# Chains of seven products: the copy of the sixth and seventh products' bank by ScalarE, and VectorE's add two steps later

## The chip, the cores and the metric

The kernel runs on one core of a Trainium2 chip. A core has a matrix engine (TensorE; PE in the profile, with PEld for its weight loads), a vector engine (VectorE, DVE), an activation engine (ScalarE, ACT), GpSimd (POOL) and SyncE (SP). TensorE writes its results into PSUM, which has eight banks of 512 fp32 columns here; VectorE and ScalarE read and write PSUM and the on-chip SBUF. Each engine takes its own instructions strictly in the order in which the program emits them, and waits at one until what it needs from other engines is done.

The metric is the device time in microseconds of one execution, the median of several runs.

## The reference

A decoder trunk of two layers over 512 tokens of width 1024, all in fp32. The first layer mixes tokens by dilated attention in three groups of eight heads, the second by a gated linear recurrence; a gated ConvFFN follows each. What matters here are the large products:

```
qkv = (x @ w_qkv)                     # 1024 x 9216, attention
u = causal_dwconv(x @ w_up, conv_w, conv_b)   # 1024 x 6144, each ConvFFN
g, v = u[..., :D_FF], u[..., D_FF:]
return (gelu(g) * v) @ w_down
```

## The kernel before

Every fp32 product is made of three faster ones: a weight or activation is split into a high part (`whi`, by ScalarE, L220) and the rest (`wlo`, by VectorE, L221), and TensorE adds up hi x hi, hi x lo and lo x hi. A weight passes through both engines before TensorE can use it.

Part of the queries and keys of the attention, and ten of the twelve column blocks of each ConvFFN's `w_up`, are multiplied by a scheme that makes a 2 x 2 block product of seven block products in place of eight. One such unit is a **chain** (`chain`, L1171 to L1206): seven products, each twelve matmuls of 256 columns, into two PSUM banks. The upper bank `y[0]` takes products 5 and 3 in its columns 256 to 511 and product 2 in columns 0 to 255. The lower bank `y[1]` takes products 1, 6, 7 and 4 in columns 0 to 255, one accumulated on the other. Between them the sums that the scheme needs are taken off: ScalarE copies products 1, 5 and 1+6 into two SBUF tiles `part` (`t[0]` and `t[1]`, L1193); VectorE adds `t[0]` to the whole upper bank (L1197); and after product 7 VectorE adds the fifth product's copy to the lower bank's sum and writes it into that bank's columns 256 to 511 (L1202). Product 4 is then accumulated onto columns 0 to 255, and the consumer takes the whole bank: in the ConvFFN ScalarE (L885) with two convolution taps on VectorE (L889), in the attention VectorE (L1304). In the traces the products of one chain are told apart by their right operand: `hT` for 1, 2 and 3, `T` for 5, 6 and 7, `last` for 4.

There are 56 chains: 16 in the attention, in four rounds of four, and 20 in each of the two ConvFFNs. Neighbouring chains overlap. The order is written out by hand: a table gives each product of a chain its step (`AT` for the ConvFFN, a new chain every `CYCLE` = 10 steps, `QUAD` for the attention, a new one every `APART` = 7), and steps without a product are filled with other products.

```
CYCLE = 10
AT = {1: 0, 5: 1, 2: 2, 6: 4, 3: 5, 7: 8, 4: 13}
APART, ROUND = 7, 44
QUAD = {1: 0, 5: 2, 2: 3, 6: 4, 3: 6, 7: 8, 4: 12}
```

A step that has a product is emitted by `slot` (L445): first the product, then everything that is due, then a `tick`, which lets side work go on and usually emits the next split of a weight (`pump`). `later(n, f)` makes `f` due n slots after the present one. So an evicting instruction stands in its engine's queue at the place of its slot, between the splits. In the ConvFFN the order of slots around a chain's end is 7, then 1, 5 and 2 of the next chain, then 4; step 9 of a cycle has no product.

Of the kernel before, what the change touches and what calls it, by code (L numbers as in the profile page):

```python
# [14 lines left out]
AF = mybir.ActivationFunctionType  # L15
ALU = mybir.AluOpType
# [118 lines left out]
def kernel(  # L135
# [25 lines left out]
    nc = tc.nc  # L161
# [23 lines left out]
    def gen(dt=F32, s="g"):  # L185
        return gp.tile([P, 512], dt, tag="g", name=nm(s))

    def psum(s="ps"):
        return pp.tile([P, 512], F32, tag="ps", name=nm(s))
# [232 lines left out]
    def chunk():  # L422
        i = state["next"]
        state["next"] += 1
        return i

    def take(i, j):
        while (i, j) not in units:
            before = len(units)
            pump(1)  # L430
            assert before != len(units), (i, j, state)
        return units[i, j]

    def done(n=2):
        state["live"] -= n
# [6 lines left out]
    def later(n, f):  # L442
        due.append([n, f])
# [727 lines left out]
    def chain(right, top, bottom):  # L1171

        i = chunk()
        y, t = {}, []

        def step(n):
            W = take(i, LEFT[n][0])
            b, at = {1: (1, 0), 6: (1, 0), 7: (1, 0), 4: (1, 0), 5: (0, 256), 3: (0, 256), 2: (0, 0)}[n]
            if b not in y:
                y[b] = psum()  # L1180
            dst = y[b][:, at : at + 256]
            for k in range(4):
                for q, (wa, ha) in enumerate(PASSES):
                    mm(  # L1184
                        dst, W[wa][0][:, k, :], right[n](ha, k), start=n in (1, 5) and k == q == 0,
                        stop=k == 3 and q == 2, skip_group_check=True,
                    )
            done(1)
            if n == 1:
                t.extend(gen(s="part") for _ in range(2))  # L1190
            if n in (1, 5, 6):
                to = {1: t[0][:, 0:256], 6: t[0][:, 256:512], 5: t[1][:, 0:256]}[n]
                later(1, lambda: nc.scalar.activation(to, dst, AF.Copy))  # L1193
            elif n == 3:

                def upper():
                    nc.vector.tensor_tensor(y[0], y[0], t[0], op=ALU.add)  # L1197
                    top(y[0])

                later(1, upper)  # L1200
            elif n == 7:
                later(1, lambda: nc.vector.tensor_tensor(y[1][:, 256:512], dst, t[1][:, 0:256], op=ALU.add))  # L1202
            elif n == 4:
                later(1, lambda: bottom(y[1]))

        return lambda n: lambda: step(n)  # L1206

    def seven(hT, T, begin, last, prep):
# [669 lines left out]
```

## Time and profile before

| | us |
|---|---|
| median of 3 runs | 1366.67 (1363.19 to 1368.01) |
| the profiled execution | 1369.2 |
| its span, first to last instruction | 1367.4 |
| TensorE busy | 1338.2 |
| VectorE busy | 1103.7 |
| ScalarE busy | 807.7 |

The granted TensorE clock is 0.997 over the span. An engine's busy time is the union of its instructions' durations. A row of the timeline gives start, duration, engine, line, operation, output and inputs with their shapes, the count of equal instructions that were merged, and in brackets the idle time before it with what ended that. Matmuls are pipelined: a matmul of 256 columns takes 0.28 us, and the next starts 0.11 after it.

### The profile page before, as it was taken

To read this page: it belongs to the slowest core of one execution; us is meant where nothing else is said; L and a number is where in the kernel's file an instruction comes from. 1 tells how busy PE (TensorE), PEld (TensorE's weight loads), DVE (VectorE), ACT (ScalarE), POOL (GpSimd) and SP (SyncE) were. 2 spreads that over 40 slices of the span, in tenths; PEclk is the share of its full clock that TensorE was granted. 3 is DMA by queue.
4 is the path that set the end of the run, shared out by engine and by line. 5 is a ranking of instruction groups with operands and counts; after the bars stand their busy time and mean duration, and the time that the engine had idled before them with its cause. 6 is when DMAs were issued, how large, how long until landed. Compare 5 with 4: busy or idle time off the path is not lost.

```text
span 1367.4 us, 24126 instructions
## 1 busy us (share of the span) xinstructions
PE 1338.2 (98%) x8981; PEld 1255.3 (92%) x8981; DVE 1103.7 (81%) x2173; ACT 807.7 (59%) x1690; POOL 236.4 (17%) x392
## 2 busy tenths in 40 slices
PE   9999999999999999999999999999999999999997
PEld 7888999889899999999999889978899999999996
DVE  6686888887876899988888759768899988888853
ACT  7343555454546476666666646489576667666641
POOL 0341341212120102221221002000102222221000
PEclk9999999999999999999999999999999999999999
DMA  7553454747483647777775542431446777776411
GB/s 231 184 148 123 124 188 122 214 109 227 120 243 99 263 155 155 183 179 175 169 169 146 174 164 81 151 109 54 162 149 148 178 182 181 178 181 163 165 68 62
DMA packets 70638, 214.53 MB, mean 157 GB/s; under 512 B 10816, under 2 KB 14360, under 8 KB 58744
## 3 DMA queue, kind: packets, MB, share of 16 engines
q1 hardware_dynamic: 42552, 153.34, 33.2%
q0 software_dynamic: 27120, 58.60, 21.2%
q8 instruction: 70, 1.15, 0.3%
q10 hardware_dynamic: 848, 1.05, 0.2%
q14 instruction: 48, 0.39, 0.1%
HBM read 193.99 MB, written 18.96 MB: 156 GB/s over the span
## 4 chain that ended last, share of the span: by engine, by line
PE 62%; issue 19%; DVE 11%; DMA 5%; ACT 3%; POOL 0%; DVEq 0%; POOLq 0%; ACTq 0%; SPq 0%
PE ps L1184 31%; PE acc L493 16%; PE ps L493 6%; PE v L1381 6%; DVE wlo L221 4%; DMA raw<-in_attn_w_qkv_dram 2%; DVE u L889 1%; DMA raw<-in_ffn_w_up_dram 1%; PE v L1319 1%; PE S L1527 1%; ACT whi L220 1%; DMA ft<-turned 1%; PE S L1475 1%; PE O L493 1%; DVE ps L1197 0%
## 5 line engine op out<-in xcount | busy, mean ns | idle before, releaser
L221 DVE TENSOR_TENSOR wlo<-raw,whi 128x512 fp32r<-128x512 f32 x628 | 417.4, 686 | 94.8 <-ACT whi L220 94.1
L220 ACT ACTIVATE whi<-raw 128x512 fp32r<-128x512 f32 x628 | 370.8, 624 | 153.1 <-PE acc L493 43.5
L1184 PE MATMUL ps<-T,whi 128*128 128x256 f32 x1344 | 235.6, 276 | 0.3
L1184 PE MATMUL ps<-hT,whi 128*128 128x256 f32 x1344 | 235.0, 276 | 0.0
L493 PE MATMUL ps<-hT,whi 128*128 128x512 f32 (+1 forms) x928 | 223.8, 334 | 0.2 <-ACT whi L220 0.2
L1184 PEld LDWEIGHTS ps<-T,whi 128*128 128x128 f32 x1344 | 207.4, 191 | 2.9 <-ACT part L1193 0.7
L1184 PEld LDWEIGHTS ps<-hT,whi 128*128 128x128 f32 x1344 | 204.3, 191 | 0.7 <-ACT part L1193 0.2
L1184 PE MATMUL ps<-T,wlo 128*128 128x256 f32 x672 | 185.3, 276 | 0.0
L1184 PE MATMUL ps<-hT,wlo 128*128 128x256 f32 x672 | 185.1, 275 | 0.0
L493 PEld LDWEIGHTS ps<-hT,whi 128*128 128x128 f32 x928 | 159.7, 190 | 13.9 <-ACT whi L220 0.4
L257 POOL DMA_DIRECT2D raw<-in_ffn_w_up_dram x120 | 104.2, 950 | 391.8 <-DVE wlo L221 308.8
L493 PE MATMUL ps<-hT,wlo 128*128 128x512 f32 (+1 forms) x464 | 154.3, 333 | 0.4 <-DVE wlo L221 0.4
L493 PE MATMUL acc<-whi,ahi 128*128 128x512 f32 x336 | 128.0, 381 | 1.8 <-DVE u L889 1.8
L493 PE MATMUL acc<-whi,alo 128*128 128x512 f32 x336 | 127.7, 380 | 1.7 <-DVE alo L221 1.6
L1184 PEld LDWEIGHTS ps<-T,wlo 128*128 128x128 f32 x672 | 128.2, 191 | 0.0
L1184 PEld LDWEIGHTS ps<-hT,wlo 128*128 128x128 f32 x672 | 128.2, 191 | 0.0
L493 PE MATMUL acc<-wlo,ahi 128*128 128x512 f32 x336 | 127.3, 379 | 0.0
L1193 ACT ACTIVATE part<-ps 128x256 f32<-128x256 f32 x168 | 63.9, 380 | 76.7 <-PE ps L1184 73.9
L1381 PE MATMUL v<-whi,hT 128*128 128x512 f32 x320 | 102.7, 384 | 0.0
L493 PEld LDWEIGHTS ps<-hT,wlo 128*128 128x128 f32 x464 | 88.3, 190 | 7.5 <-DVE wlo L221 0.6
L1184 PE MATMUL ps<-last,whi 128*128 128x256 f32 x448 | 79.5, 278 | 6.5 <-DVE ps L1202 6.5
L889 DVE SCALAR_TENSOR_TENSOR u<-ps,cols,u 128x511 f32<-128x511 f32 x112 | 83.5, 746 | 2.0
(227 smaller groups left out, 2453.3 us busy)
## 6 DMA issues: line engine op xcount, KB each, us to landing
raw<-in_ffn_w_up_dram SPq DMA_DIRECT2D x48, 1024.0 KB
raw<-in_attn_w_qkv_dram SPq DMA_DIRECT2D x34, 1024.0 KB
raw<-in_ffn_w_up_dram POOLq DMA_DIRECT2D x120, 256.0 KB, 5.6
raw<-in_ffn_w_down_dram SPq DMA_DIRECT2D x14, 1024.0 KB
dw<-in_ffn_w_down_dram SPq DMA_DIRECT2D x40, 256.0 KB
raw<-in_lru_w_in_dram SPq DMA_DIRECT2D x8, 1024.0 KB
turned<-T POOLq DMA_DIRECT2D x26, 256.0 KB, 2.6
ft<-turned POOLq DMA_DIRECT2D x104, 64.0 KB, 4.9
```

Source lines behind the costliest of these rows:

```text
L220: nc.scalar.activation(hi, raw, AF.Copy)
L221: nc.vector.tensor_tensor(lo, raw, hi.bitcast(F32), op=ALU.subtract)
L257: nc.gpsimd.dma_start(blocks(i)[to], plan[i][3][0][0][:, 4 * b : 4 * b + 4, :], accum_op=ALU.add)
L493: mm(dst, l[a], r[b], start=start and n == 0, stop=stop and n == 2)
L889: nc.vector.scalar_tensor_tensor(u[:, d:], ps[:, : S - d], wc, u[:, d:], op0=ALU.mult, op1=ALU.add)
L1184: mm(dst, W[wa][0][:, k, :], right[n](ha, k), start=n in (1, 5) and k == q == 0, stop=k == 3 and q == 2, skip_group_check=True,)
L1193: later(1, lambda: nc.scalar.activation(to, dst, AF.Copy))
L1319: mm(banks[t], hT[a][:, k, t * P : (t + 1) * P], two(W[b][k % 2][:, 0, :]), start=u == n == 0, stop=u == 3 and n == 5,)
L1381: mm(bank, hT[a][:, k, t * P : (t + 1) * P], two(W[b][k % 2][:, 0, :]), start=(k, a, b) == (0, 0, 0), stop=(k, a, b) == (KD - 1, 1, 0),)
L1475: mm(Sp[a // 2][:, o + lo : o + 256], q[hh][:, a * P : (a + 1) * P], k[hh][:, k0 : (a + 1) * P], start=True, stop=True)
L1527: mm(ps[:, c], q[hh][:, c], k[hh][:, c], start=True, stop=True)
```

## The change

The sum of the first, sixth and seventh products is no longer read out of PSUM by VectorE's add. One slot after product 7, where the add stood, ScalarE copies it into the free half of the tile `t[1]`. Two slots later VectorE adds the fifth product's copy to that copy, both from SBUF, and writes the result to the same columns 256 to 511 of the lower bank. All 56 chains are changed alike; nothing else is.

```diff
             elif n == 7:
-                later(1, lambda: nc.vector.tensor_tensor(y[1][:, 256:512], dst, t[1][:, 0:256], op=ALU.add))
+                p5, u7 = t[1][:, 0:256], t[1][:, 256:512]
+                later(1, lambda: nc.scalar.activation(u7, dst, AF.Copy))
+                later(3, lambda: nc.vector.tensor_tensor(y[1][:, 256:512], u7, p5, op=ALU.add))
             elif n == 4:
                 later(1, lambda: bottom(y[1]))
```

## The prediction

> **What bounds the kernel now.** I read the page first, then stretches of the span, the groups by shape, and at last the timeline of one engine at a time around a seventh product.
>
> ```profile
> span 1367.4 us, 24126 instructions
> PE 1338.2 (98%) x8981; PEld 1255.3 (92%) x8981; DVE 1103.7 (81%) x2173; ACT 807.7 (59%) x1690; POOL 236.4 (17%) x392
> ...
> 562.33:742.03 179.70, 179.70 (x1443) 176.10 (x1441) 158.72 (x256) 120.26 (x225) 38.24 (x44) 1.00 0.72 175
> 150.00:415.00 265.00, 258.69 (x1955) 248.47 (x1954) 217.48 (x493) 132.06 (x332) 68.21 (x125) 1.00 0.57 171
> ```
>
> TensorE bounds it: 29.2 us of the span are not PE. In the steady part of the first ConvFFN (15 chains; the columns are length, PE, PEld, DVE, ACT, POOL, clock, DMA) PE is never idle, so whatever makes it wait there is added to the time whole. VectorE is next, 88% busy; ScalarE is 67% busy. In the attention chains PE is idle for 6.3 us of 265.
>
> ```profile
> L1202 DVE TENSOR_TENSOR ps<-ps,part 128x256 f32<-128x256 f32 x56 | 23.8, 426 | 0.0
> L1504 DVE TENSOR_TENSOR plo<-ft,phi 128x256 fp32r<-128x256 f32 x8 | 3.3, 418 | 0.0
> L1193 ACT ACTIVATE part<-ps 128x256 f32<-128x256 f32 x168 | 63.9, 380 | 76.7 <-PE ps L1184 73.9 <-DVE plo L1504 0.9
> L885 ACT ACTIVATE u<-ps,cols,neg 128x512 f32<-128x512 f32 x40 | 31.3, 783 | 3.0 <-PE ps L1184 3.0
> L1184 PE MATMUL ps<-last,whi 128*128 128x256 f32 x448 | 79.5, 278 | 6.5 <-DVE ps L1202 6.5
> ```
>
> L1202 is the add that the change moves; there are 56, one a chain. The last row is the fourth product, which accumulates onto what L1202 read. It waited for L1202 five times, 6.5 us in all. That is everything the change could win on TensorE.
>
> **The instructions.** 56 copies come onto ScalarE, priced by L1193: 56 x 0.380 = 21.3 us. The add reads its two inputs from SBUF; the nearest row of its size is L1504, 0.418 against 0.426 us, so I keep 0.43. Neither cost lies on TensorE. In the steady part the copy stands ahead of L909, for which ScalarE waits 1.21 us (row at 584.19 below), which hides it; without that cover it would cost 0.38 a chain at most. No DMA moves, and nothing is moved past SP's or POOL's queue. The `part` buffer is held two slots longer; no row of before waits for one, so I add nothing. What matters is the place of the add and who waits for it.
>
> The Trainium skill (Perfetto Trace Analysis, Optimizing Scalar/DVE Operations) puts VectorE's access overhead at about 60 ns in SBUF and 125 ns in PSUM. By that the add would be 65 ns shorter, an estimate from the page, and the sum about 3 us smaller; the rows above show 8 ns.
>
> **Where the add comes to stand.** A slot emits one product, then what is due, then one weight split. L1202 is due one slot after the seventh product; the fourth product comes four slots after it. The new add is due three slots after, so it is emitted directly ahead of the fourth product, behind the splits of two more slots. The question is whether the fourth product waits for it: it writes columns 0 to 255 of the bank, the add columns 256 to 511.
>
> ```profile
> 584.61 0.39 PE L1184 MATMUL ps<-T,whi 128*128 128x256 f32 x2
> ...
> 584.95 0.39 PE L1184 MATMUL ps<-hT,whi 128*128 128x256 f32 x2
> ...
> 586.17 0.28 PE L1184 MATMUL ps<-hT,wlo 128*128 128x256 f32 x1
> 586.28 0.39 PE L1184 MATMUL ps<-last,whi 128*128 128x256 f32 x2
> ...
> 584.19 0.63 ACT L909 ACTIVATE u<-u 128x512 f32<-128x512 f32 x1 [1.21 <-DVE u L889]
> 584.73 0.37 ACT L1193 ACTIVATE part<-ps 128x256 f32<-128x256 f32 x1
> 584.99 0.62 ACT L220 ACTIVATE whi<-raw 128x512 fp32r<-128x512 f32 x1
> 586.49 0.39 ACT L1193 ACTIVATE part<-ps 128x256 f32<-128x256 f32 x1 [0.88 <-PE ps L1184]
> ```
>
> The copy at 586.49 takes the fifth product, columns 256 to 511 of the upper bank, finished at about 585.1. It sat idle until the second product (operand hT, columns 0 to 255 of the same bank) ended at 586.17 + 0.28. So an engine waits for whoever was ordered before it in the bank, whatever the columns. I take the same for a product behind an add: the fourth product waits. No row shows that direction, so the other answer is a rival.
>
> The Trainium skill (PSUM — Partial Sum Buffer, PSUM bank collisions raise a hardware error) has the rule that bears on that direction: PSUM is guarded by bank and quadrant, "not by address". By the rule the wait is there; by addresses alone it would not be.
>
> **What a wait costs.** VectorE's rows of two neighbouring chains (the fourth products were to start at 586.28 and, 11.99 later, 598.27):
>
> ```profile
> 584.61 0.43 DVE L1202 TENSOR_TENSOR ps<-ps,part 128x256 f32<-128x256 f32 x1
> 584.94 1.39 DVE L221 TENSOR_TENSOR wlo<-raw,whi 128x512 fp32r<-128x512 f32 x2
> 587.42 0.69 DVE L221 TENSOR_TENSOR wlo<-dw,whi 128x512 fp32r<-128x512 f32 x1 [1.09 <-ACT whi L220]
> ...
> 596.59 0.43 DVE L1202 TENSOR_TENSOR ps<-ps,part 128x256 f32<-128x256 f32 x1
> 596.92 0.68 DVE L221 TENSOR_TENSOR wlo<-raw,whi 128x512 fp32r<-128x512 f32 x1
> 597.52 0.69 DVE L913 TENSOR_TENSOR u<-u,u 128x512 f32<-128x512 f32 x1
> 598.12 0.69 DVE L221 TENSOR_TENSOR wlo<-raw,whi 128x512 fp32r<-128x512 f32 x1
> ...
> 598.27 0.39 PE L1184 MATMUL ps<-last,whi 128*128 128x256 f32 x2
> ...
> 549.77 0.43 DVE L1202 TENSOR_TENSOR ps<-ps,part 128x256 f32<-128x256 f32 x1
> 551.31 0.68 DVE L221 TENSOR_TENSOR wlo<-raw,whi 128x512 fp32r<-128x512 f32 x1
> ...
> 550.25 0.49 PE L1184 MATMUL ps<-last,whi 128*128 128x256 f32 x2 [1.41 <-DVE ps L1202]
> ```
>
> First kind: the second L221 ends at 586.33; it can't come earlier, since its whi ends at 584.99 + 0.62. The add starts 0.10 before that end, as neighbours here overlap, and ends at 586.66. The row at 550.25 shows the product 0.05 behind the add it waits for: 586.71, so 0.43 late. Second kind: the three instructions behind L1202 move forward by the 0.33 that it held (596.59 to 596.92), so the last ends at 598.48; the add, 0.10 before that, ends at 598.81; 0.05 on is 598.86, so 0.59 late. The row at 550.25 also shows what a restart costs: two products take 0.49 in place of 0.39, 0.10 more.
>
> Does VectorE catch up while TensorE waits? What comes next in its chain:
>
> ```profile
> 575.53 0.28 PE L1184 MATMUL ps<-last,wlo 128*128 128x256 f32 x1
> ...
> 575.85 0.79 ACT L885 ACTIVATE u<-ps,cols,neg 128x512 f32<-128x512 f32 x1
> 576.53 0.61 ACT L220 ACTIVATE whi<-raw 128x512 fp32r<-128x512 f32 x1
> ...
> 577.25 0.69 DVE L221 TENSOR_TENSOR wlo<-raw,whi 128x512 fp32r<-128x512 f32 x1
> ```
>
> ScalarE's L885 starts 0.04 after the fourth product ends, L220 behind it, and VectorE takes L220's result 0.11 later. So a late fourth product makes VectorE late too, but for some 0.08, and the next wait comes again: 0.35 and 0.51, with restarts 0.45 and 0.61, 1.06 for two chains. If VectorE were not held, one wait would pay for the next and two chains would cost 0.59 + 0.10 = 0.7.
>
> **The sum.** Sixteen chains of each ConvFFN (third to eighteenth) are of this kind: 8 x 1.06 = 8.5 us. The first two start behind a full VectorE queue: the second's L221 ends at 551.99 (L1202's 0.33 leaves ahead of it, the first chain's add comes in), its own add 0.33 later, then 0.05, so 552.37 against 550.25: 2.1 for both. The nineteenth:
>
> ```profile
> 753.58 1.29 DVE L221 TENSOR_TENSOR wlo<-raw,whi 128x512 fp32r<-128x512 f32 x2
> ...
> 754.01 0.39 PE L1184 MATMUL ps<-last,whi 128*128 128x256 f32 x2
> ...
> 240.12 0.69 DVE L315 TENSOR_TENSOR raw<-raw 128x512 f32<-128x512 f32 x1
> ...
> 238.66 0.39 PE L1184 MATMUL ps<-last,whi 128*128 128x256 f32 x2
> ...
> 309.97 0.69 DVE L319 TENSOR_TENSOR raw<-raw 128x512 f32<-128x512 f32 x1
> ...
> 309.40 0.28 PE L1184 MATMUL ps<-last,whi 128*128 128x256 f32 x1
> ...
> 275.06 0.50 PE L1184 MATMUL ps<-last,whi 128*128 128x256 f32 x2 [2.01 <-DVE ps L1202]
> 343.83 0.38 PE L1184 MATMUL ps<-last,whi 128*128 128x256 f32 x1 [1.26 <-DVE ps L1202]
> ```
>
> 754.87 + 0.33 + 0.05 is 1.24 late; less 0.08, with restart, 1.3. The twentieth's add falls behind its fourth product: nothing. One ConvFFN: 8.5 + 2.1 + 1.3 = 11.9, both 23.8 us.
>
> Attention has 16 chains in four rounds. The instruction behind which the add stands gives 240.81 + 0.38 - 238.66 = 2.5 us late for the chain at 238.66, and 310.66 + 0.38 - 309.40 = 1.6 for the one at 309.40. The same reading of every chain gives nine that wait, 0.9 to 2.5 each, some 14 before any catching up and 15 with restarts; the fourth chain of a round has nothing queued between and doesn't wait longer. In rounds two and three the fourth chain waited already (2.01 and 1.26, last rows): there the lost time is partly what is lost now. Following these waits along each round I come to an estimate of 3.2, 3.3, 2.1 and 1.7, so 10; the bounds are 3, if most is swallowed by such waits and by transfers of weights, and 15. I take 9, near the estimate.
>
> Together 33 us. The profiled execution took 1369.2 us for its span of 1367.4, 2.5 over the median of the three, 1366.67; a difference goes onto either. **1366.7 + 33 = 1399 us.**
>
> **Rivals.**
> - *Columns decide, not banks.* The fourth product waits for the copy alone and the 6.5 us of waits go: 1360 us, the faster side. It decides from the first chain on. Against it stands the copy at 586.49; for it, that no row shows a product behind an add to other columns. 0.08.
> - *VectorE catches up.* Two chains cost 0.7, the ConvFFNs 2 x (5.6 + 3.4) = 18, attention 3: 1388 us. For it: VectorE is idle 1.09 before 587.42. Against: that idle ends by whi, behind the copy at 586.49, not by the add. 0.20.
> - *ScalarE's order.* The new copy waits for the seventh product and holds the splits behind it where ScalarE runs ahead, in attention; 0.38 for each of 16 chains more: 1405 us. 0.08.
> - *The add is in time*, because VectorE runs earlier than I read: 1367 us. It needs half a microsecond in every chain. 0.06.
>
> **How the numbers follow.** My forecast has 0.58, for 1390 to 1410. What this kernel's measurement can tell from no change is about 0.3%, 4 us. Slower: 0.58 + 0.20 + 0.08 = 0.86; same 0.06; faster 0.08. The range 1380 to 1412 leaves out the two cheap cases, 0.14, and a little of the tails.
>
> **What would show it.** Right: the groups name a wait of the fourth product (operand last) for the new add's line, some 30 us over about 45 chains, its matmuls 0.1 longer at each; the steady stretch grows from 179.7 by about 8 us; ScalarE gains 56 copies of 0.38 and TensorE's wait for them is near nothing. Wrong: fourth products that start while the add still runs (the first rival), or waits in every second chain alone (the second). A clock under 1.00 or longer matmuls in the steady stretch would mean that I looked in the wrong place.

## The result and the profile after

The change makes the kernel slower: 1404.28 us, median of 4 runs (1401.36 to 1406.68), against 1365.69 us for the kernel before beside it (4 runs). The ratio is 1.0278, with a 95% interval of 1.0259 to 1.0297. On a second chip it was 1404.67 against 1367.75, ratio 1.0270 [1.0255, 1.0285]. The span grew from 1367.4 to 1402.7 us, by 35.3, at a granted clock of 0.996 (0.997 before), so the clock isn't where the time went.

The first lines of the page of the changed kernel:

```profile
span 1402.7 us, 24204 instructions
PE 1347.5 (96%) x8981; PEld 1260.3 (90%) x8981; DVE 1108.1 (79%) x2173; ACT 830.3 (59%) x1746; POOL 236.6 (17%) x392
```

TensorE has the same 8981 matmuls, but 55.2 us of its span are idle in place of 29.2. VectorE has the same 2173 instructions; ScalarE has 56 instructions and 22.6 us more.

The groups by shape of the changed kernel, where the copy is line L1203 and the add L1204 (output, input, shapes, count, busy, mean ns, idle time before them and what ended it):

```profile
L1184 PE MATMUL ps<-last,whi 128*128 128x256 f32 x448 | 82.5, 285 | 35.4 <-DVE ps L1204 24.8 <-ACT part L1193 7.5 <-ACT whi L220 3.1
L1204 DVE TENSOR_TENSOR ps<-part 128x256 f32<-128x256 f32 x56 | 23.9, 426 | 0.6 <-ACT part L1203 0.6
L1203 ACT ACTIVATE part<-ps 128x256 f32<-128x256 f32 x56 | 21.3, 381 | 11.0 <-PE ps L1184 7.8
```

The fourth product (operand `last`) is where the idle time stands: 35.4 us in place of 6.5. The waits of TensorE split it by the instruction that came last:

```profile
PE ps L1184 <- DVE ps L1204: 24.8, 29, 2.1
PE ps L1184 <- ACT part L1193: 7.5, 16, 0.5
PE ps L1184 <- ACT whi L220: 3.1, 2, 1.7
```

That is 29 + 16 + 2 = 47 waits, one in nearly every chain. The 16 put down to a copy of ScalarE (L1193) are a question of naming: in each of them VectorE's add ended 0.15 us ahead of the product, as in those that are named for the add. The two put down to L220 are of the same kind.

The stretch of 15 chains that was 179.70 us long, between the same two products, and the attention stretch, in the windows view (length, PE, PEld, DVE, ACT, POOL, clock, DMA share, GB/s):

```profile
574.10:763.27 189.17, 183.21 (x1440) 177.22 (x1441) 160.29 (x255) 126.98 (x242) 37.38 (x43) 1.00 0.68 166
150.00:420.00 270.00, 255.73 (x1913) 245.55 (x1912) 215.20 (x488) 134.98 (x344) 68.63 (x125) 0.99 0.55 165
```

The steady stretch grew by 9.47 us, at full clock. In the attention's window TensorE is idle for 14.3 us of 270, where it was idle for 6.3 of 265. One wait of the steady stretch, in the timelines of VectorE and TensorE (the fourth product that started at 586.28 before), and the fourth products ahead of it and behind it:

```profile
598.13 0.69 DVE L221 TENSOR_TENSOR wlo<-raw,whi 128x512 fp32r<-128x512 f32 x1 [0.36 <-ACT whi L220]
598.74 0.43 DVE L1204 TENSOR_TENSOR ps<-part 128x256 f32<-128x256 f32 x1
599.97 0.69 DVE L221 TENSOR_TENSOR wlo<-dw,whi 128x512 fp32r<-128x512 f32 x1 [0.80 <-ACT whi L220]
...
586.78 0.46 PE L1184 MATMUL ps<-last,whi 128*128 128x256 f32 x2 [0.47 <-ACT part L1193]
...
598.72 0.28 PE L1184 MATMUL ps<-hT,wlo 128*128 128x256 f32 x1
599.31 0.46 PE L1184 MATMUL ps<-last,whi 128*128 128x256 f32 x2 [0.32 <-DVE ps L1204]
...
612.00 0.46 PE L1184 MATMUL ps<-last,whi 128*128 128x256 f32 x2 [0.47 <-ACT part L1193]
```

The second product's last matmul starts at 598.72. Unhindered, the fourth product would start 0.11 later; the add that stands behind a weight split runs until 599.17, and it starts at 599.31. Two things are to be read here. First, the gap from 598.72 is 0.59, but the idle time in brackets only 0.32: while the last matmul runs out alone, TensorE counts as busy. That is why the idle time of the group understates the loss and TensorE's busy time rose by 9.3 us with the same matmuls. Second, the loss is better read from the starts: 586.78, 599.31, 612.00 are 12.53 and 12.69 apart, where they were 11.98 on average (574.31, 586.28 and 598.27 before). Each pair of chains loses 0.55 + 0.71 = 1.26 us.

Added up in this manner over all 56 fourth products, the lag is 9.5 us at the end of the attention, 12.9 over the first ConvFFN and 13.0 over the second: 35.3 before rounding, the whole of the span's growth. One thing is hidden in the 9.5: the first matmul of the chains starts at 150.24 before and at 148.75 after. Counted from there, the attention's chains lost 11.0 us in this pair of traces.

### The profile page after: what moved, and what is told of

It is laid out like the page before. It is cut to its first block, busy times and chain, and to the rows that moved or that the text cites. A ratio compares the mean times of both kernels' runs of the same rounds, so it can differ in the third digit from the quotient of the medians.

```text
span 1402.7 us, 24204 instructions
## 1 busy us (share of the span) xinstructions
PE 1347.5 (96%) x8981; PEld 1260.3 (90%) x8981; DVE 1108.1 (79%) x2173; ACT 830.3 (59%) x1746; POOL 236.6 (17%) x392
## 4 chain that ended last, share of the span: by engine, by line
PE 52%; issue 22%; DVE 11%; ACT 7%; DMA 5%; POOL 1%; SPq 0%; DVEq 0%; POOLq 0%; ACTq 0%
PE ps L1184 24%; PE acc L493 13%; PE v L1383 6%; PE ps L493 5%; DVE wlo L221 4%; DVE u L889 3%; ACT whi L220 3%; ACT u L885 2%; DMA raw<-in_ffn_w_up_dram 2%; DMA ft<-turned 1%; DVE ps L1197 1%; ACT part L1193 1%; DVE ps L1204 1%; PE S L1529 1%; ACT u L909 1%
## 5 line engine op out<-in xcount | busy, mean ns | idle before, releaser
L220 ACT ACTIVATE whi<-raw 128x512 fp32r<-128x512 f32 x628 | 374.3, 624 | 142.8 <-PE ps L1184 41.1
L1184 PE MATMUL ps<-last,whi 128*128 128x256 f32 x448 | 82.5, 285 | 35.4 <-DVE ps L1204 24.8
L1193 ACT ACTIVATE part<-ps 128x256 f32<-128x256 f32 x168 | 63.7, 379 | 85.7 <-PE ps L1184 81.6
L1184 PEld LDWEIGHTS ps<-last,whi 128*128 128x128 f32 x448 | 68.4, 191 | 43.3 <-ACT whi L220 14.8
```

Source lines behind the costliest of these rows:

```text
L220: nc.scalar.activation(hi, raw, AF.Copy)
L1184: mm(dst, W[wa][0][:, k, :], right[n](ha, k), start=n in (1, 5) and k == q == 0, stop=k == 3 and q == 2, skip_group_check=True,)
```

## The experiments

The theory: the fourth product is held by the add that is emitted ahead of it in its bank, so the add's place costs the time, by 0.45 and 0.61 us in the steady chains. The rivals: the copy on ScalarE costs it; VectorE's extra distance or load costs it; the columns alone decide.

### The place alone, and the copy alone

`place_only` moves the add and makes no copy; it reads PSUM as before. (The last chain of each ConvFFN has its fourth product ahead of the moved add, so there the sum that is read holds that product too.)

```diff
-                later(1, lambda: nc.vector.tensor_tensor(y[1][:, 256:512], dst, t[1][:, 0:256], op=ALU.add))
+                later(3, lambda: nc.vector.tensor_tensor(y[1][:, 256:512], dst, t[1][:, 0:256], op=ALU.add))
```

> Before's add, still reading the sum out of PSUM, emitted three slots after the seventh product in place of one; no copy by ScalarE. Theory of the place and the bank: the fourth product waits for the add as in the changed kernel, so 1398 to 1408 us and a wait of the fourth product for line L1202 of some 25 to 35 us. Theory of the copy (the time goes with ScalarE's 56 copies): within 0.3% of before, 1362 to 1370 us.

`copy_only` leaves the add where it was and adds the copy, which nothing reads.

```diff
+                later(1, lambda: nc.scalar.activation(t[1][:, 256:512], dst, AF.Copy))
                 later(1, lambda: nc.vector.tensor_tensor(y[1][:, 256:512], dst, t[1][:, 0:256], op=ALU.add))
```

> Before with ScalarE's 56 copies added where the change has them; nobody reads the copies, and VectorE's add stays as it was. Theory of the place: 1363 to 1370 us, since 21 us of copies lie in ScalarE's idle time. Theory of the copy: most of the 38 us, 1390 us or more.

The place alone: 1401.55 us against 1366.07, ratio 1.0255 [1.0223, 1.0286]. The copy alone: 1364.61, ratio 1.0003 [0.9984, 1.0022]. The fourth product's group, first with the place alone, then with the copy alone:

```profile
L1184 PE MATMUL ps<-last,whi 128*128 128x256 f32 x448 | 84.8, 290 | 30.6 <-DVE ps L1202 30.6
```

```profile
L1184 PE MATMUL ps<-last,whi 128*128 128x256 f32 x448 | 79.6, 278 | 5.0 <-DVE ps L1204 5.0
L1203 ACT ACTIVATE part<-ps 128x256 f32<-128x256 f32 x56 | 21.5, 383 | 7.2 <-PE ps L1184 6.2
```

The copies lie wholly beside other work: 21.5 us more on ScalarE, no time that shows. The move gives nearly the whole loss, and here all of the wait is named for the add.

### The same extra work of VectorE, into the bank and into SBUF

Both kernels have ScalarE's copy, as the change has it, keep the add in its old place and do it a second time at the new one. `again_bank` writes the bank, `again_sbuf` writes a tile in SBUF that nothing reads.

```diff
                 later(1, lambda: nc.vector.tensor_tensor(y[1][:, 256:512], dst, t[1][:, 0:256], op=ALU.add))
+                later(3, lambda: nc.vector.tensor_tensor(y[1][:, 256:512], u7, p5, op=ALU.add))   # again_bank
+                later(3, lambda: nc.vector.tensor_tensor(p5, u7, p5, op=ALU.add))                 # again_sbuf
```

> Before's add at its place, ScalarE's copy, and the changed kernel's add three slots on as well, which writes the same values into the same columns of the lower bank once more. Place and bank: the fourth product waits for the second add, and VectorE has 0.33 us more ahead of it than in the changed kernel: 1404 to 1425 us. Theory that only VectorE's time at that place counts: the same as the kernel whose second add writes to SBUF.

> As the kernel with the add made twice, but the second add writes its result into the SBUF tile part (nobody reads it) and not into the bank. VectorE does the same work at the same place. Place and bank: no wait of the fourth product for it, 1365 to 1374 us (the 24 us of adds lie in VectorE's idle time but for the heads of the ConvFFNs). Theory of VectorE's time: 1400 us or more, as the kernel that writes to the bank.

Into the bank: 1409.07 us, ratio 1.0314 [1.0278, 1.0349]. Into SBUF: 1367.79, ratio 1.0004 [0.9983, 1.0026]. The groups of the two, in this order (the second add is L1205):

```profile
L1184 PE MATMUL ps<-last,whi 128*128 128x256 f32 x448 | 86.1, 293 | 35.7 <-DVE ps L1205 35.7
```

```profile
L1184 PE MATMUL ps<-last,whi 128*128 128x256 f32 x448 | 79.5, 278 | 6.9 <-DVE ps L1204 6.9
L1204 DVE TENSOR_TENSOR ps<-ps,part 128x256 f32<-128x256 f32 x56 | 23.8, 426 | 3.2 <-ACT part L1203 3.2
L1205 DVE TENSOR_TENSOR part<-part 128x256 f32<-128x256 f32 x56 | 23.4, 419 | 0.1
```

VectorE has 56 more instructions in the same place of its queue in both, 23.4 and 23.9 us. They cost nothing where they write elsewhere and 43.0 us (1409.07 - 1366.07) where they write the bank's other half. So neither VectorE's load nor its order costs the time; the wait for the bank does, though the two instructions touch different columns.

### Half the distance

`one_step` makes the add due two slots behind the seventh product in place of three.

```diff
-                later(3, lambda: nc.vector.tensor_tensor(y[1][:, 256:512], u7, p5, op=ALU.add))
+                later(2, lambda: nc.vector.tensor_tensor(y[1][:, 256:512], u7, p5, op=ALU.add))
```

> The changed kernel with the add two slots after the seventh product in place of three, so one step after the copy. In the steady part of the ConvFFN one or two splits then stand behind the add and not ahead of it: the add of the first kind of chain would end near 585.7, before the fourth product at 586.28, that of the second kind near 597.9 to 598.2 against 598.27, so the waits go or shrink to 0.1. Place and bank: 1366 to 1380 us. Theory of the copy: no change from the changed kernel, 1400 to 1408 us.

1374.85 us against 1367.25, ratio 1.0069 [1.0045, 1.0093]: one slot earlier takes away some three quarters of the loss (0.69% is left of 2.70 to 2.78%). TensorE's waits, a steady chain in the timelines, and the last chain of the first ConvFFN:

```profile
PE ps L1184 <- DVE ps L1204: 11.5, 10, 2.2
...
597.78 0.43 DVE L1204 TENSOR_TENSOR ps<-part 128x256 f32<-128x256 f32 x1
...
598.15 0.28 PE L1184 MATMUL ps<-hT,wlo 128*128 128x256 f32 x1
598.36 0.46 PE L1184 MATMUL ps<-last,whi 128*128 128x256 f32 x2
...
767.75 0.46 PE L1184 MATMUL ps<-last,whi 128*128 128x256 f32 x2 [1.84 <-DVE ps L1204]
```

In the steady chains the add is now nearly in time: in this one it ends at 598.21, and the product starts 0.21 after the matmul ahead of it, 0.10 late; in every other one the product starts 0.11 after it, not late at all. Most of the wait that is left lies at the heads and ends of the ConvFFNs: the second chain of each waits 2.23, and the twentieth, shown here, 1.84, since its add now stands ahead of its fourth product.

### The ConvFFNs alone, the attention alone

```diff
-                later(1, lambda: nc.vector.tensor_tensor(y[1][:, 256:512], dst, t[1][:, 0:256], op=ALU.add))
+                if moved:    # True in the ConvFFN's chains alone, or in the attention's alone
+                    p5, u7 = t[1][:, 0:256], t[1][:, 256:512]
+                    later(1, lambda: nc.scalar.activation(u7, dst, AF.Copy))
+                    later(3, lambda: nc.vector.tensor_tensor(y[1][:, 256:512], u7, p5, op=ALU.add))
+                else:
+                    later(1, lambda: nc.vector.tensor_tensor(y[1][:, 256:512], dst, t[1][:, 0:256], op=ALU.add))
```

> The change in the 40 chains of the ConvFFNs alone; the 16 attention chains as before. By the prediction's terms +24 us; by the shift of the fourth products in the changed kernel's profile (35.3 us in all, 9.5 of them by the end of the attention) +26 us and more for the whole of it: 1388 to 1394 us.

> The change in the 16 attention chains alone. By the prediction's term and by the shift in the changed kernel's profile +9 us: 1373 to 1378 us. If waits in the attention were swallowed by later waits, within 0.3% of before.

ConvFFNs alone: 1392.07 us, ratio 1.0188 [1.0161, 1.0215], so 25.7 us (0.0188 x 1367.25), 22.0 to 29.4. Attention alone: 1379.21, ratio 1.0087 [1.0057, 1.0118], so 11.9, 7.8 to 16.1, a little above the 1373 to 1378 us that were expected. Together 37.6, within the intervals as much as the whole change: the two parts add up. A single pair of traces is a poor measure of the attention, because the unchanged attention differs between executions. Its window in the kernel that changes the ConvFFNs alone:

```profile
150.00:415.00 265.00, 262.45 (x1978) 252.11 (x1977) 218.33 (x518) 132.23 (x335) 69.29 (x127) 1.00 0.57 170
```

TensorE is idle for 2.5 us of it, where the same attention in the kernel before left 6.3. Several traces together tell more. The table has the time from the first matmul of the chains to the fourth product of a round's last chain, then from round to round, in four traces whose attention has the add in its old place (the kernel before, `copy_only`, `again_sbuf`, the ConvFFNs alone) and in three that have the change there (the change, the change repeated below, the attention alone):

| round, us | one | two | three | four |
|---|---|---|---|---|
| add in its old place | 54.2 to 54.4 | 66.7 to 70.6 | 68.0 to 69.7 | 66.5 |
| changed | 61.3 to 63.0 | 70.0 to 71.9 | 69.3 to 69.6 | 68.2 to 68.4 |

Rounds one and four are steady enough to compare: they lose 7.0 to 8.8 and 1.7 to 1.9 us. Over all four rounds the two means are 13.7 us apart.

### What the copy adds: an instruction on TensorE's queue

The change was 35.3 us longer in its trace, the place alone 32.7. Behind the add the fourth product starts 0.15 us later in the one and 0.05 to 0.06 in the other. A view of the chains' line shows what differs, for the changed kernel (over the span, then within the wait above), and for the kernel before:

```profile
L1184 PEldq EVENT_SEMAPHORE  x94: 51/51/51, 146.7 to 1309.0; - x94
...
L1184 PEldq EVENT_SEMAPHORE  x1: 51/51/51, 599.2 to 599.2; - x1
```

```profile
L1184 PEldq EVENT_SEMAPHORE  x44: 51/51/51, 148.2 to 1269.1; - x44
```

TensorE's queue holds 50 more semaphore instructions of 51 ns ahead of weight loads. The Trainium skill (Perfetto Trace Analysis, Identifying Dependency Chains) says that an instruction that waits for several engines may get such instructions put ahead of it with the further conditions; the counts fit that. To tell whether the copy costs its 0.38 us on ScalarE or this instruction, four kernels ran on one chip: the change, the place alone, the place with a copy that nothing reads (where VectorE stays the last reader of the columns that the fourth product writes over), and one for the next part.

```diff
+                later(1, lambda: nc.scalar.activation(t[1][:, 256:512], dst, AF.Copy))
-                later(1, lambda: nc.vector.tensor_tensor(y[1][:, 256:512], dst, t[1][:, 0:256], op=ALU.add))
+                later(3, lambda: nc.vector.tensor_tensor(y[1][:, 256:512], dst, t[1][:, 0:256], op=ALU.add))   # place_copy
```

> The change once more, beside the move of the add without the copy and the move with a copy that nobody reads, all on one chip, to tell what the copy itself adds. In the traces so far the fourth product starts 0.15 us behind the add with the change and 0.05 to 0.06 with the move alone, and the products of the chains show 94 semaphore instructions ahead of their weight loads in place of 44. Theory (an extra semaphore instruction is the cost, since the fourth product now writes over columns that ScalarE read last): about 36 to 39 us over the kernel before, 2 to 3 us above the move alone. Rival (what differs is chance between executions): no difference from the move alone.

> The add moved two slots later, reading PSUM as before, without a copy. (In the last chain of each ConvFFN the moved add comes behind the fourth product, so there it reads a sum with the fourth product in it; the rest of the work is the same.) Theory: 33 to 36 us over the kernel before, 2 to 3 us below the change. Rival: the same as the change.

> The move alone and beside it ScalarE's copy one slot after the seventh product, which nothing reads; the add reads PSUM. (The last chain of each ConvFFN as in the move alone.) It has the change's work on ScalarE and the add's place, but VectorE is the last reader of the columns that the fourth product writes over. Theory (extra semaphore instruction): 44 semaphore instructions, the fourth product 0.05 to 0.06 behind the add, the time of the move alone within 1.5 us. Rival (the copy's 0.38 us on ScalarE costs the 2 to 3 us, by holding weight splits behind it): the time of the change.

| | us | runs from, to | ratio [95%] | semaphore instructions |
|---|---|---|---|---|
| the change | 1404.67 | 1402.72, 1405.82 | 1.0270 [1.0255, 1.0285] | 94 |
| the place and an unread copy | 1401.29 | 1400.65, 1402.15 | 1.0248 [1.0234, 1.0261] | 44 |
| the place alone | 1400.06 | 1398.41, 1401.75 | 1.0238 [1.0223, 1.0253] | 44 |

The place alone, in its windows and timelines (the same stretch and the same chain as above):

```profile
573.56:761.74 188.18, 183.65 (x1440) 177.16 (x1440) 160.26 (x255) 122.75 (x227) 37.39 (x43) 1.00 0.68 167
...
598.16 0.43 DVE L1202 TENSOR_TENSOR ps<-ps,part 128x256 f32<-128x256 f32 x1
...
586.18 0.49 PE L1184 MATMUL ps<-last,whi 128*128 128x256 f32 x2 [0.37 <-DVE ps L1202]
...
598.64 0.49 PE L1184 MATMUL ps<-last,whi 128*128 128x256 f32 x2 [0.22 <-DVE ps L1202]
...
611.26 0.49 PE L1184 MATMUL ps<-last,whi 128*128 128x256 f32 x2 [0.38 <-DVE ps L1202]
```

The starts are 12.46 and 12.62 apart: 0.48 and 0.64 over 11.98, 1.12 a pair. The unread copy, with the same ScalarE work as the change, has the same pair and the 44 instructions, and stands 3.4 us below the change. So the copy's time on ScalarE isn't most of it: the unread copy stands 1.2 us above the place alone, and their intervals overlap widely. The intervals of the change and of the unread copy overlap by a little (1.0255 to 1.0261), their runs do not. The distance from the change to the place alone, 4.6 us, is more than the 2 to 3 that were expected.

The traces tell it wait by wait. In the change, in its repeat and in the kernels that change one part alone, every fourth product that waits for its moved add has a semaphore instruction 0.11 us ahead of its start, and starts 0.14 to 0.15 behind the add. In the kernel before, the place alone, the unread copy and `again_bank`, none that waits has one, and they start 0.05 to 0.06 behind. `one_step` has both in one kernel: 25 products are held until 0.15 behind their add, all with the instruction, and one, at 272.76, starts 0.06 behind, without it. Where nothing is waited for, the instruction costs nothing that shows: there the product starts 0.11 after the matmul ahead, with it or without. In a steady chain it costs 0.07 (0.55 and 0.71 for 0.48 and 0.64); 47 waits make 3.3 us. No kernel was run that differs from the change in this instruction alone.

### The add behind the fourth product

`behind` keeps the copy and puts the add into the fourth product's slot, behind it and ahead of the consumer.

```diff
+                later(1, lambda: nc.scalar.activation(t[1][:, 256:512], dst, AF.Copy))
-                later(1, lambda: nc.vector.tensor_tensor(y[1][:, 256:512], dst, t[1][:, 0:256], op=ALU.add))
             elif n == 4:
+                later(0, lambda: nc.vector.tensor_tensor(y[1][:, 256:512], t[1][:, 256:512], t[1][:, 0:256], op=ALU.add))
                 later(1, lambda: bottom(y[1]))
```

> ScalarE's copy as in the change; VectorE's add emitted directly behind the fourth product (in the same slot) in place of directly ahead of it, so the fourth product waits for the copy alone and the add for the fourth product. Place and bank: the waits for the add vanish, also before's 6.5 us, and ScalarE's L885 waits for the add by some 0.6 us a chain: 1357 to 1368 us. Theory of the copy: 1400 us or more.

> The copy one slot after the seventh product, VectorE's add in the slot of the fourth product and behind it, ahead of the consumer of the bank. The fourth product then has no add ahead of it in the bank. Theory: 7 to 9 us under the kernel before (ratio 0.993 to 0.995): the five waits of 6.5 us and their restarts go, and nothing takes their place, since the consumer stands behind the fourth product anyway. Rival (the gain seen before was chance between executions): within 3 us of the kernel before.

1358.95 us against 1367.25, ratio 0.9943 [0.9918, 0.9968]; again on the other chip 1359.74 against 1367.75, ratio 0.9947 [0.9933, 0.9961]. It is faster than both kernels, by 8 us than the one before and by 45 than the change. Its groups, a stretch of 15 chains and the last 14 of them, then the same 14 of the kernel before:

```profile
L1184 PE MATMUL ps<-last,whi 128*128 128x256 f32 x448 | 78.8, 277 | 0.0
L885 ACT ACTIVATE u<-ps,cols,neg 128x512 f32<-128x512 f32 x40 | 31.3, 782 | 33.5 <-DVE ps L1204 33.5
L1204 DVE TENSOR_TENSOR ps<-part 128x256 f32<-128x256 f32 x56 | 24.0, 428 | 9.4 <-PE ps L1184 9.3
...
551.96:732.15 180.19, 179.97 (x1442) 176.20 (x1441) 161.80 (x258) 122.65 (x243) 38.21 (x44) 1.00 0.72 175
564.43:732.15 167.72, 167.72 (x1346) 164.38 (x1345) 150.79 (x241) 113.28 (x224) 35.61 (x41) 1.00 0.72 175
```

```profile
574.31:742.03 167.72, 167.72 (x1347) 164.37 (x1345) 148.26 (x239) 112.19 (x210) 35.27 (x41) 1.00 0.71 174
```

The fourth product waits for nothing now: the 6.5 us that it waited for the add before are gone. The wait has moved to the consumer, where ScalarE's L885 stands 33.5 us for the add. That costs almost nothing: in the 14 chains TensorE isn't idle at all, and they are as long as before to the hundredth. The chain ahead of them takes 12.47 us in place of 11.98, so the 15 take 180.19 where they took 179.70; TensorE waits there once for a copy of ScalarE (0.23 us, L1193, ahead of a product with operand `T`). The same chain of the second ConvFFN is as long.

## Why the prediction was right, and where its sizes were off

**The bound and the place.** Right. TensorE's idle time set the end, the add came to stand directly ahead of the fourth product, and the product waited for it across columns. The last was an inference from a copy behind a product; the trace of the change and the two adds with different destinations show the other direction. The lower bank is one tile of the program and fills one bank, so the runs don't tell whether the order is kept by tile or by bank. The Trainium skill's rule (PSUM — Partial Sum Buffer, PSUM bank collisions raise a hardware error) of guarding by bank and not by address agrees: adds into the other half of the bank cost 43 us, into SBUF nothing. Whether the chip itself would stall without the program's semaphore wasn't tried, since two engines would then touch one bank unguarded.

**The sum.** 1366.7 + 33 is 1399.7, where the forecast says 1399. The measured growth is 38.6 us (1404.28 over 1365.69), 5.6 more than the 33. Two terms were mis-sized: one wait in the ConvFFNs, worth some 2 us, and the attention, which has most of the rest.

**One wait.** The first of them is "add to product 0.05", taken from the row at 550.25. It measured 0.15 with the change, where the product had an instruction more on its queue; the restart came to 0.07 in place of 0.10. Without the copy the row was a good one: 0.05, restart 0.10, and 0.48 and 0.64 against the 0.45 and 0.61 of the prediction. With it 0.55 and 0.71, so 1.26 a pair and not 1.06. In the trace the sixteen chains of a ConvFFN lost 9.9 us where the sum has 8.5, so 2.8 us too little in both.

**No catching up.** Right. Every chain of a ConvFFN from the third to the nineteenth lost time, none paid for the next. The row at 599.97 shows why: VectorE is idle 0.80 us behind the add, for `whi`, exactly where the prediction put it.

| term, us | predicted | measured |
|---|---|---|
| steady stretch of 15 chains | about 8 | 9.47 |
| first two chains of a ConvFFN | 2.1 | 1.8 and 2.0 |
| nineteenth | 1.3 | 1.14 |
| twentieth | 0 | 0 |
| both ConvFFNs | 23.8 | 25.9 in the trace, 25.7 timed alone |
| attention | 9, bounds 3 and 15 | 11.0 in the trace from the first chain on, 13.7 between means of several traces, 11.9 timed alone |

**The attention.** The value lies within its bounds, but it is too small, and the round that missed is the first: 3.2 predicted, 7.0 to 8.8 in the traces. Its first three fourth products alone left TensorE idle for 5.75 us in the change, against 0.60 before. Which reading made the 3.2 too small stays open, since the prediction gives the rounds without their working. The fourth round is right, 1.7 for 1.7 to 1.9. The second and third (3.3 and 2.1) can't be confirmed: the unchanged attention moves there by as much as what is sought. The 9.5 at the end of the attention, counted from the start of the span, is near the 9 by luck. What held was that the fourth chains of rounds two and three stopped waiting: the waits of 2.01 and 1.26 are gone.

**The copies and the add.** Right at nothing for ScalarE's time: the copy alone costs none that shows. The rival in which ScalarE's order adds 0.38 a chain is out, though its 1405 us is nearer to the measured time than the forecast. Reading SBUF in place of PSUM, and still writing PSUM, didn't shorten the add: 0.426 both times; writing SBUF too, it took 0.419. The 65 ns that the Trainium skill's figures would give (Perfetto Trace Analysis, Optimizing Scalar/DVE Operations) do not show.

**The rivals.** "Columns decide" is out, but its price was good: 6.5 us of waits gone, 1360 us. The kernel with the add behind the product gets just that, 1358.95 and 1359.74, by order and not by columns. "VectorE catches up" (1388) and "the add is in time" (1367) are out; the second shows what it would have taken, since one slot earlier the steady chains are in time but for 0.10.

## What to carry to other kernels

In this kernel, where two engines share a PSUM bank, an instruction waits for what was emitted ahead of it in that bank, whatever the columns; so put an eviction either well ahead of the next product, or behind it if only a later consumer needs the result. Cost a moved instruction at its new place in its own engine's queue, behind what is queued there, and ask whether the pacing engine is next in line. And count the engines that an instruction on the pacing engine waits for: a second one can cost an instruction on its queue, here 0.1 us in each wait, 0.07 with the cheaper restart.

## What the runs showed that was not expected

A copy whose time is hidden on its own engine still cost some 3 us on TensorE, which goes with 50 semaphore instructions of 51 ns ahead of weight loads; the same copy, unread, brought none of them and stood 1.2 us above the place alone, within the noise. The idle time of a group understates a wait on a pipelined engine: 0.32 in the row at 599.31, 0.55 in the distance of the products. And the kernel before held a gain in the other direction, 0.5%, for the add three slots later than it stands there, behind the product.
